# The tail, norm and first block of three chained products, worked by token halves

## The chip, the cores and the metric

One core of a Trainium2 chip. The metric is the device time of one execution in microseconds (us). TensorE is called PE here, VectorE DVE, ScalarE ACT; SP is the engine that issues the weight DMAs.

## The reference

One conditioned decoder layer on 256 tokens of width 2048, in fp32: a SwiGLU FFN (hidden width 5632), a pair of token mixers behind one wide projection, a second FFN, and a last norm. Each of the three sub-layers starts with an RMSNorm that is scaled and shifted by vectors computed from c.

```python
x = x + 1/2 * gate1(c) * SwiGLU1(mod1(RMSNorm(x)))
h = mod2(RMSNorm(x)); p = h @ w_in                 # 2048 x 13312
x = x + gate2(c) * ((sig(g_ret) * y_ret + sig(g_swa) * y_swa) @ w_out)
x = x + 1/2 * gate3(c) * SwiGLU2(mod3(RMSNorm(x)))
out = RMSNorm(x) * norm_final
mod(h) = h * (1 + scale(c)) + shift(c);  [shift, scale, gate] x 3 = c_act @ w_ada + b_ada
SwiGLU(h) = (silu(h @ w_gate) * (h @ w_up)) @ w_down
```

## The kernel before

**Products.** Tokens lie in two halves t of 128. Each fp32 product is three PE matmuls: high part by high part (L288), low by high (L289), high by low (L290). A weight tile is 512 x 512 (1 MB): `load` issues its DMA on SP into one of four `raw` buffers; ACT casts its high part `wh` in two pieces of 128x1024 (L296), and DVE subtracts to get the low part `wl` (L297). The split pieces live in `wsp`, three buffers of each kind. The activation side is split either once for all (`Held`, tiles `hh` and `hl`) or as it is used (`Whole.pair`, tile `a`: ACT L327, DVE L328). `gemm` walks the contraction in steps of four blocks of 128 (a "kb"); for each tile it runs both token halves, 24 matmuls. The down products (ffn1 down, w_out, ffn2 down) are worked in two passes of two column blocks of 512.

**Background.** The vectors for shift, scale and gate come from `ada`: 1 MB of `w_ada` into a `raw` buffer and four DVE reductions (L195) per step. `gemm` starts such steps at the given `rate`, so they stand among the product's own work on DVE and SP.

**Boundaries.** After a down product's second pass, `add_gated` scales each half's PSUM bank (L442), adds it to x (L443) and lets ACT sum its squares (L381). Then one `inv_rms` for both halves (reduce L385, square root on ACT L369, four DVE steps), then `norm`: per 256 columns and half a DVE scaling (L416), PE transposes (L420), a DVE modulation from PSUM (L401, 128x256), ACT's `hh` (L404) and DVE's `hl` (L405). There are two such boundaries, from ffn1 down to w_in and from w_out to the second FFN; behind ffn2 down the last norm writes the output (L895, DMA L903).

**Order.** Every engine runs its own instructions strictly in a fixed order. SP's is the program's; that of the others is set when the kernel is built. An instruction that waits holds up all that stand behind it on its engine.

```python
for p in range(2):
    c0s = [(2 * p + i) * CH for i in range(2)]
    banks = gemm(act, w, c0s, KT=KF, rate=rate)
    for b, c0 in zip(banks, c0s):
        add_gated(b, c0, gate, ssq)
```

## Time and profile before

| | |
|---|---|
| median of 3 runs | 2516.82 us (2515.35 to 2518.6) |
| the profiled execution | 2512.52 us |
| its span | 2510.7 us |
| mean granted PE clock | 0.992 |
| PE busy | 2431.5 us, 97% of the span |
| DVE busy | 1712.6 us, 68% |
| ACT busy | 1172.6 us, 47% |

The span runs from the first to the last instruction that the profile shows; 1.8 us of the profiled execution lie outside it. PE has work in 97% of the span, so what a change can take back on PE's side is idle time and time at a low clock.

### The profile page before, as it was taken

To read this page: it belongs to the slowest core of one execution; us is meant where nothing else is said; L and a number is where in the kernel's file an instruction comes from. 1 tells how busy PE (TensorE), PEld (TensorE's weight loads), DVE (VectorE), ACT (ScalarE), POOL (GpSimd) and SP (SyncE) were. 2 spreads that over 40 slices of the span, in tenths; PEclk is the share of its full clock that TensorE was granted. 3 is DMA by queue.
4 is the path that set the end of the run, shared out by engine and by line. 5 is a ranking of instruction groups with operands and counts; after the bars stand their busy time and mean duration, and the time that the engine had idled before them with its cause. 6 is when DMAs were issued, how large, how long until landed. Compare 5 with 4: busy or idle time off the path is not lost.

```text
span 2510.7 us, 29247 instructions
## 1 busy us (share of the span) xinstructions
PE 2431.5 (97%) x10910; PEld 1977.4 (79%) x10910; DVE 1712.6 (68%) x2843; ACT 1172.6 (47%) x1566; POOL 5.7 (0%) x14
## 2 busy tenths in 40 slices
PE   6999999999997999999999999998999999999997
PEld 4778888788786877777888888886788888888886
DVE  7997776668877766776766776766756554445655
ACT  5445444344444454455444454455444444444443
POOL 0000000000000000000000000000000000000000
PEclk9999999999998999999999999999999999999999
DMA  9995787788786655555667777765566665555553
GB/s 361 361 341 202 250 291 296 278 292 300 268 299 241 230 204 185 194 184 193 226 246 254 246 273 252 280 213 189 184 235 245 225 251 187 197 187 190 196 185 116
DMA packets 243472, 599.08 MB, mean 239 GB/s; under 512 B 9537, under 2 KB 9921, under 8 KB 224001
## 3 DMA queue, kind: packets, MB, share of 16 engines
q1 hardware_dynamic: 242402, 591.61, 66.4%
...
HBM read 595.06 MB, written 2.12 MB: 238 GB/s over the span
## 4 chain that ended last, share of the span: by engine, by line
PE 91%; DVE 6%; DMA 1%; ACT 1%; issue 1%; SPq 0%; ACTq 0%; DVEq 0%
PE pa L290 29%; PE pa L289 29%; PE pa L288 29%; DVE wl L297 2%; PE ps L361 1%; DVE slot L195 1%; DMA raw<-in_w_ada_dram 1%; DVE raw L195 1%; PE pd L639 1%; PE pd L636 0%; ACT wh L296 0%; PE pd L701 0%; PE pd L361 0%; DVE slot L572 0%; DMA x_sb<-in_x_dram 0%
## 5 line engine op out<-in xcount | busy, mean ns | idle before, releaser
L297 DVE TENSOR_TENSOR wl<-raw,wh 128x1024 fp32r<-128x1024 f32 x842 | 1014.0, 1211 | 644.5 <-ACT wh L296 641.5
L296 ACT CAST wh<-raw 128x1024 fp32r<-128x1024 f32 x842 | 878.2, 1043 | 1130.9 <-PE pa L289 1101.3
L289 PE MATMUL pa<-wh,hl 128*128 128x512 f32 x2240 | 878.4, 392 | 1.1 <-DVE hl L405 1.1
L288 PE MATMUL pa<-wh,hh 128*128 128x512 f32 x2240 | 871.0, 393 | 5.6 <-ACT hh L404 2.1
L290 PE MATMUL pa<-wl,hh 128*128 128x512 f32 x2240 | 817.1, 394 | 8.1 <-DVE wl L297 7.7
L290 PEld LDWEIGHTS pa<-wl,hh 128*128 128x128 f32 x2240 | 418.7, 188 | 104.4 <-DVE wl L297 17.2
L288 PEld LDWEIGHTS pa<-wh,hh 128*128 128x128 f32 x2240 | 421.4, 188 | 99.6 <-ACT wh L296 4.5
L289 PEld LDWEIGHTS pa<-wh,hl 128*128 128x128 f32 x2240 | 421.6, 188 | 90.7 <-issue 2.8
L289 PE MATMUL pa<-wh,a 128*128 128x512 f32 x1088 | 423.4, 390 | 3.2 <-DVE a L328 3.2
L288 PE MATMUL pa<-wh,a 128*128 128x512 f32 x1088 | 403.6, 391 | 1.3 <-ACT wh L296 0.9
L290 PE MATMUL pa<-wl,a 128*128 128x512 f32 x1088 | 403.2, 390 | 0.1
L289 PEld LDWEIGHTS pa<-wh,a 128*128 128x128 f32 x1088 | 204.5, 188 | 47.2 <-DVE a L328 4.6
L288 PEld LDWEIGHTS pa<-wh,a 128*128 128x128 f32 x1088 | 204.2, 188 | 45.9 <-ACT wh L296 2.2
L290 PEld LDWEIGHTS pa<-wl,a 128*128 128x128 f32 x1088 | 204.6, 188 | 43.1 <-DVE wl L297 0.9
L195 DVE CUSTOM_DVE_ANT_0 raw<-raw,cact 128x512 f32<-128x512 f32 x336 | 214.6, 687 | 0.0
L195 DVE CUSTOM_DVE_ANT_0 raw<-raw,cact,bcols 128x512 f32<-128x512 f32 x112 | 83.9, 749 | 85.0 <-DMA raw<-in_w_ada_dram 84.8
L328 DVE TENSOR_TENSOR a<-slot,a 128x512 fp32r<-128x512 f32 x136 | 93.1, 685 | 0.0
L327 ACT CAST a<-slot 128x512 fp32r<-128x512 f32 x136 | 83.9, 618 | 0.0
L195 DVE CUSTOM_DVE_ANT_0 slot<-slot,cact 128x512 f32<-128x512 f32 x96 | 61.5, 689 | 0.0
L362 ACT COPY slot<-ps 128x512 f32<-128x512 f32 x80 | 43.9, 588 | 35.4 <-PE ps L361 35.1
L195 DVE DVE_READ_ACCUMULATOR2_ANT sums<- 128x1 f32 x576 | 48.0, 83 | 0.0
L361 PE MATMUL ps<-small_c,t 128*128 128x128 f32 x288 | 38.9, 273 | 0.0
...
## 6 DMA issues: line engine op xcount, KB each, us to landing
raw<-in_w_ffn_gu_dram SPq DMA_DIRECT2D x156, 1024.0 KB, 4.9
raw<-in_w_ada_dram SPq DMA_DIRECT2D x112, 1024.0 KB, 4.9
raw<-in_w_in_dram SPq DMA_DIRECT2D x104, 1024.0 KB, 5.0
raw<-in_w_ffn_down_dram SPq DMA_DIRECT2D x88, 1024.0 KB, 5.1
slot<-in_w_ada_dram SPq DMA_DIRECT2D x32, 1024.0 KB, 8.0
raw<-in_w_swa_branch_dram SPq DMA_DIRECT2D x16, 1024.0 KB, 5.2
raw<-in_w_ret_branch_dram SPq DMA_DIRECT2D x16, 1024.0 KB, 5.3
raw<-in_w_out_dram SPq DMA_DIRECT2D x16, 1024.0 KB, 5.1
```

The lines of the kernel that those rows point to most:

```text
L195: nc.vector.tensor_tensor_reduce(out=w[:, at], in0=w[:, at], in1=cact[:, at], scale=1.0, scalar=bcols[:, m, k : k + 1] if q == 0 else 0.0, ...
L288: nc.tensor.matmul(ps, ah[:, j, ts], wh[:, j, :], start=first, stop=False)
L289: nc.tensor.matmul(ps, al[:, j, ts], wh[:, j, :], start=False, stop=False)
L290: nc.tensor.matmul(ps, ah[:, j, ts], wl[:, j, :], start=False, stop=last)
L296: nc.scalar.copy(hi, src)
L297: nc.vector.tensor_sub(lo, src, hi.bitcast(F32))
L327: nc.scalar.copy(hi, v)
L328: nc.vector.tensor_sub(lo, v, hi.bitcast(F32))
L361: nc.tensor.transpose(ps[:, j * P : (j + 1) * P], src_of(j), ident)
L362: nc.any.tensor_copy(dest, ps[:, : n * P])
L639: nc.tensor.matmul(ps[:, P : 3 * P], qo[hs, pair, P:], skt[hs, kv, :], start=True, stop=True)
```

## The change

The last pass of a down product ends in `gemm_tail`: of its last two steps a and b, the first tile is run whole, and the three others, (a, second column block), (b, first), (b, second), are split but kept: two of them in 16 KB buffers of the slot pool ("home" tiles), the last in `wsp`, and the activations of step b in a home tile as well. Then half 0 of all three is multiplied, then half 1. `add_gated` and the norm follow per half: `norm_half` for the two boundaries, `final` at the end. `gemm_head` does the same for the first block of the next product: its four tiles are kept split (three in homes, the last in `wsp`); half 0 is multiplied as soon as its norm is there, half 1 later. `inv_rms` now takes one half; its square root adds the epsilon by itself, and `root_table` is a square root of a constant in front of each down product. The scaling by the norm is on ACT (L517, 128x512), the modulation alternates by 128 columns between DVE (L531) and ACT (L529), and `hh`/`hl` are made per half for four blocks at once (L537, L538). Some background rates differ (0.55 to 0.6 in the first FFN's up product, 0.36 to 0.375 in w_in, 0.25 to 0 in ffn2 down), and no background step is started in the last two steps of a tail or in a head. The number of matmuls is the same.

```diff
-    def products(banks, ah, al, wh, wl, starts, ends):
+    def products(banks, ah, al, wh, wl, starts, ends, halves=range(NT)):
         n = ah.shape[1]
         for j in range(n):
             first, last = starts and j == 0, ends and j == n - 1
-            for t in range(NT):
+            for t in halves:
...
+        def pair(self, k2, home=None):
             t = self.tiles[k2 * 2 // KD]
             j = (2 * k2) % KD
             v = t.rearrange("p (k s) -> p k s", s=S)[:, j : j + 2, :]
-            both = pair_tile()
+            if home is None:
+                home = pair_tile()
...
+    def home_tile():
+        return slots.tile([P, 2, KD * P], F32R, tag="slot", name=nm("home"))
...
+    def halves_of(w, kb, c0, home=None):
+        raw = load(w, kb, c0)
+        pairs = []
+        for h in range(2):
+            src = raw[:, 2 * h : 2 * h + 2, :]
+            if home is None:
+                pairs.append(split(wsp, "w", src, CH))
+                continue
+            hi, lo = (
+                home[:, i].rearrange("p (k n) -> p k n", n=CH)[:, 2 * h : 2 * h + 2, :]
+                for i in range(2)
+            )
+            nc.scalar.copy(hi, src)
+            nc.vector.tensor_sub(lo, src, hi.bitcast(F32))
+            pairs.append((hi, lo))
+        return pairs
...
+    def gemm_tail(act, w, col0s, KT, rate):
+        banks = [[acc_bank() for _ in range(NT)] for _ in col0s]
+        nb = KT // KB
+        for kb in range(nb - 2):
+            credit[0] += rate * len(col0s)
+            n = int(credit[0])
+            credit[0] -= n
+            gemm_part(act, w, col0s, banks, kb, KT)
+            tick(n)
+        a, b = nb - 2, nb - 1
+        pairs = {a: [act.pair(a * 2 + h) for h in range(2)]}
+        for h, (wh, wl) in enumerate(halves_of(w, a, col0s[0])):
+            products(banks[0], *pairs[a][h], wh, wl, False, False)
+        steps = [(a, 1, halves_of(w, a, col0s[1], home_tile()))]
+        home = home_tile().rearrange("p i n -> p (i n)")
+        pairs[b] = [
+            act.pair(
+                b * 2 + h,
+                home[:, h * 2 * CH : (h + 1) * 2 * CH].rearrange("p (i n) -> p i n", i=2),
+            )
+            for h in range(2)
+        ]
+        steps.insert(0, (b, 0, halves_of(w, b, col0s[0], home_tile())))
+        steps.append((b, 1, halves_of(w, b, col0s[1])))
+        def last(t):
+            for kb, i, parts in steps:
+                for h, (wh, wl) in enumerate(parts):
+                    products(
+                        banks[i], *pairs[kb][h], wh, wl, False, kb == b and h == 1, [t]
+                    )
+        last(0)
+        return banks, lambda: last(1)
...
+    def gemm_head(w, c0, held):
+        banks = [acc_bank() for _ in range(NT)]
+        nb = KD // KB
+        steps = []
+        def products_of(kb, parts, t):
+            for h, (wh, wl) in enumerate(parts):
+                k2 = kb * 2 + h
+                products(
+                    banks, *held.pair(k2), wh, wl, k2 == 0, 2 * k2 + 2 == KD, [t]
+                )
+        for kb in range(nb):
+            parts = halves_of(w, kb, c0, home_tile() if kb < nb - 1 else None)
+            steps.append((kb, parts))
+            products_of(kb, parts, 0)
+        def rest():
+            for kb, parts in steps:
+                products_of(kb, parts, 1)
+        return banks, rest
...
+    def root_table():
+        nc.scalar.activation(small(1, "root"), eps, AF.Sqrt)
...
+    def inv_rms(ssq, t):
+        s = small(1, "sum")
+        v = small(1, "var")
+        r = small(1, "rs1")
+        q = small(1, "rq1")
         nc.vector.tensor_reduce(
-            out=v, in_=ssq.rearrange("p (t c) -> p t c", t=NT), axis=AX.X, op=ALU.add
-        )
+            out=s, in_=ssq[:, t * 4 : (t + 1) * 4], axis=AX.X, op=ALU.add
+        )
+        nc.scalar.activation(r, s, AF.Sqrt, bias=eps, scale=1.0 / D)
...
+        nc.vector.reciprocal(r, r)
+        nc.vector.scalar_tensor_tensor(
+            out=q, in0=v, scalar=r, in1=r, op0=ALU.mult, op1=ALU.mult
+        )
+        nc.vector.tensor_scalar(
+            out=q, in0=q, scalar1=-0.5, scalar2=1.5, op0=ALU.mult, op1=ALU.add
+        )
+        nc.vector.tensor_mul(r, r, q)
+        return r
...
+    def norm_half(held, ssq, t, m_shift):
+        r = inv_rms(ssq, t)
+        ts = slice(t * P, (t + 1) * P)
+        for kb in range(KD // KB):
+            xn = t512()
+            xs = x_sb[:, t, kb * CH : (kb + 1) * CH]
+            nc.scalar.mul(xn, xs, r)
+            ps = bank()
+            h = t512()
+            for j in range(KB):
+                js = slice(j * P, (j + 1) * P)
+                nc.tensor.transpose(ps[:, js], xn[:, js], ident)
+            for j in range(KB):
+                js = slice(j * P, (j + 1) * P)
+                k = kb * KB + j
+                scale = modc[:, m_shift + 1, k : k + 1]
+                shift = modc[:, m_shift, k : k + 1]
+                if j % 2:
+                    nc.scalar.activation(h[:, js], ps[:, js], AF.Identity, bias=shift, scale=scale)
+                else:
+                    nc.vector.tensor_scalar(
+                        out=h[:, js], in0=ps[:, js], scalar1=scale, scalar2=shift,
+                        op0=ALU.mult, op1=ALU.add,
+                    )
+            h4 = h.rearrange("p (k s) -> p k s", s=P)
+            hi = held.hi[:, kb * KB : (kb + 1) * KB, ts]
+            nc.scalar.copy(hi, h4)
+            nc.vector.tensor_sub(
+                held.lo[:, kb * KB : (kb + 1) * KB, ts], h4, hi.bitcast(F32)
...
-    def add_gated(banks, c0, gate, ssq):
+    def add_gated(banks, c0, gate, ssq, halves=range(NT)):
+        for t in halves:
...
-    def ffn_up(held, w, tiles, first, rate):
+    def ffn_up(held, w, tiles, first, rate, bg=None):
         for ci in range(first, DFF // CH):
-            bg = gemm(held, w, [ci * CH], rate=rate)[0]
+            bg = bg or gemm(held, w, [ci * CH], rate=rate)[0]
             bu = gemm(held, w, [DFF + ci * CH], rate=rate)[0]
             swiglu_up(bg, bu, tiles, ci)
-    def ffn_down(tiles, w, gate, rate):
+            bg = None
...
+    def down_product(act, w, gate, KT, rate, half_done):
         ssq = small(NT * 4, "ssq")
-        act = Whole(tiles)
-        for p in range(2):
-            c0s = [(2 * p + i) * CH for i in range(2)]
-            banks = gemm(act, w, c0s, KT=KF, rate=rate)
+        root_table()
+        c0s = [0, CH]
+        banks = gemm(act, w, c0s, KT=KT, rate=rate)
+        for b, c0 in zip(banks, c0s):
+            add_gated(b, c0, gate, ssq)
+        c0s = [2 * CH, 3 * CH]
+        banks, rest = gemm_tail(act, w, c0s, KT, rate)
+        rest()
+        for t in range(NT):
             for b, c0 in zip(banks, c0s):
-                add_gated(b, c0, gate, ssq)
-        return ssq
+                add_gated(b, c0, gate, ssq, [t])
+            half_done(ssq, t)
...
+    def into_norm(m_shift, w):
+        held = Held()
+        box = []
+        def half_done(ssq, t):
+            norm_half(held, ssq, t, m_shift)
+            if t == 0:
+                box.extend(gemm_head(w, 0 if m_shift == 6 else O_SK, held))
+            else:
+                box.pop()()
+        return held, box, half_done
...
-    ffn_up(held, gu, tiles, 5, 0.55)
+    ffn_up(held, gu, tiles, 5, 0.6)
     gate_load(gate, 2)
-    ssq = ffn_down(tiles, dn, gate, 0.55)
-    need(4, 3)
-    held = norm(ssq, 3)
     wi = w_in[0]
+    held, head, half_done = into_norm(3, wi)
+    down_product(Whole(tiles), dn, gate, KF, 0.55, half_done)
+    assert {3, 4} <= done
     dec = one.tile([P, D], F32, tag="row", name="dec")
     nc.gpsimd.dma_start(dec, consts[:, C_DEC:])
-    MR = 0.36
+    MR = 0.375
...
-    b = in_chunk(O_SK)
+    b = head[0]
...
-    for p in range(2):
-        c0s = [(2 * p + i) * CH for i in range(2)]
-        banks = gemm(a_m, w_out[0], c0s)
-        for b, c0 in zip(banks, c0s):
-            add_gated(b, c0, gate, ssq)
     need(7, 6)
-    held = norm(ssq, 6)
+    held, head, half_done = into_norm(6, w_ffn2_gu[0])
+    down_product(a_m, w_out[0], gate, KD, 0.0, half_done)
...
+    ffn_up(held, w_ffn2_gu[0], tiles, 0, 0.25, head[:1][0])
...
+    def final(ssq, t):
+        r = inv_rms(ssq, t)
+        for ci in range(4):
+            cs = slice(ci * CH, (ci + 1) * CH)
             o = t512()
...
+    down_product(Whole(tiles), w_ffn2_down[0], gate, KF, 0.0, final)
```

ACT at the boundary from ffn1 down to w_in. Before, from the table load for the square root on (`rs2` is the inverse RMS of both halves, `t` a modulated block):

```order
L369 ACT_TABLE_LOAD
L369 ACTIVATE rs2_1062_5958<-var_1061_5955 128x2
L404 CAST hh_1064_5966<-t_1069_5977 128x256
L404 CAST hh_1064_5966<-t_1070_5981 128x256
L404 CAST hh_1064_5966<-t_1074_5994 128x256
```

Now, from the table load of half 0 on (`home` and `wh` on the left are high parts of w_in's first block; 1085 is its last tile, 1119 the next block's first; `t_1062`, `t_1065`, `t_1068` are the scaled x; `hh_753` the first high part that PE can use):

```order
L482 ACT_TABLE_LOAD
L482 ACTIVATE rs1_1060_5957<-sum_1058_5955,eps_100 128x1
L377 CAST home_1078_6043<-raw_1079_6044 128x1024 x2
L377 CAST home_1080_6062<-raw_1081_6063 128x1024 x2
L517 ACTIVATE t_1062_5966<-x_sb_91,rs1_1060_5957 128x512
L298 CAST wh_1085_6087<-raw_1082_6081 128x1024
L298 CAST wh_1119_6269<-raw_1118_6267 128x1024
L517 ACTIVATE t_1065_5980<-x_sb_91,rs1_1060_5957 128x512
L529 ACTIVATE t_1064_5969<-ps_1063_5968,modc_129 128x128
L517 ACTIVATE t_1068_5994<-x_sb_91,rs1_1060_5957 128x512
L529 ACTIVATE t_1064_5969<-ps_1063_5968,modc_129 128x128
L537 CAST hh_753_4154<-t_1064_5969 128x4x128
```

Four casts of kept weights (two rows x2) stand between half 0's square root and its first scaling of x, and the first `hh` stands behind two modulations by ACT.

DVE at the same place. Before, from the last step of the inverse RMS on:

```order
L376 TENSOR_TENSOR rs2_1062_5958<-rs2_1062_5958,rq2_1063_5959 128x2
L416 TENSOR_SCALAR t_1067_5969<-x_sb_91,rs2_1062_5958 128x256
L416 TENSOR_SCALAR t_1068_5973<-x_sb_91,rs2_1062_5958 128x256
L401 TENSOR_SCALAR t_1069_5977<-ps_1066_5968,modc_127 128x256
L401 TENSOR_SCALAR t_1070_5981<-ps_1066_5968,modc_127 128x256
L416 TENSOR_SCALAR t_1072_5986<-x_sb_91,rs2_1062_5958 128x256
L416 TENSOR_SCALAR t_1073_5990<-x_sb_91,rs2_1062_5958 128x256
L405 TENSOR_TENSOR hl_1065_5967<-t_1069_5977,hh_1064_5966 128x256
L405 TENSOR_TENSOR hl_1065_5967<-t_1070_5981,hh_1064_5966 128x256
```

Now, from the step behind half 0's inverse RMS on (`home` low parts of the kept tiles, the two modulations of the first four blocks of 128 columns, one background step on `raw_1123`, of which six like rows are left out, and the first `hl`):

```order
L378 TENSOR_TENSOR home_1078_6043<-raw_1079_6044,home_1078_6043 128x1024 x2
L378 TENSOR_TENSOR home_1080_6062<-raw_1081_6063,home_1080_6062 128x1024 x2
L531 TENSOR_SCALAR t_1064_5969<-ps_1063_5968,modc_129 128x128
L299 TENSOR_TENSOR wl_1086_6088<-raw_1082_6081,wh_1085_6087 128x1024
L299 TENSOR_TENSOR wl_1120_6270<-raw_1118_6267,wh_1119_6269 128x1024
L531 TENSOR_SCALAR t_1064_5969<-ps_1063_5968,modc_129 128x128
L197 ISA raw_1123_6301,sums_1022_5717<-raw_1123_6301,cact_105,bcols_119 128x512
...
L197 ISA sums_1022_5717 128x1
L531 TENSOR_SCALAR t_1067_5983<-ps_1066_5982,modc_129 128x128
L538 TENSOR_TENSOR hl_754_4155<-t_1064_5969,hh_753_4154 128x4x128
```

Where before nothing stood between the inverse RMS and the first `hl` but the norm's own rows, there are now four low parts of homes, two of `wl`, and a background step.

ACT in w_out's second pass, at its second step of four. Before (`wh_2349` and `wh_2351` are the two pieces of that step's first tile, `a_2346` and `a_2347` its activations, `t` the sums of squares of the first pass):

```order
L296 CAST wh_2349_12973<-raw_2348_12971 128x1024
L381 ACTIVATE t_2327_12880,ssq_2269_12566<-x_sb_91 128x512
L381 ACTIVATE t_2329_12885,ssq_2269_12566<-x_sb_91 128x512
L296 CAST wh_2351_12989<-raw_2348_12971 128x1024
L327 CAST a_2346_12965<-slot_1943_10622 128x512
L296 CAST wh_2354_13007<-raw_2353_13005 128x1024
```

Now (`wh_2332` and `wh_2334` are that tile's pieces, `a_2329` its first activations; `home_2348` is the kept tile of the third step, second column block; `home_2350` the activations of the fourth step):

```order
L298 CAST wh_2332_12969<-raw_2331_12967 128x1024
L467 ACTIVATE t_2310_12876,ssq_2251_12560<-x_sb_91 128x512
L467 ACTIVATE t_2312_12881,ssq_2251_12560<-x_sb_91 128x512
L377 CAST home_2348_13075<-raw_2349_13076 128x1024 x2
L330 CAST home_2350_13082<-slot_1922_10608 128x512 x2
L298 CAST wh_2334_12985<-raw_2331_12967 128x1024
L330 CAST a_2329_12961<-slot_1922_10608 128x512
L298 CAST wh_2337_13003<-raw_2336_13001 128x1024
```

The casts of a tile two steps ahead and of the last step's activations stand in front of the activations that PE needs next. `raw_2349` is loaded into the buffer that `raw_2324`, the second tile of the step before, leaves free. DVE's rows keep the same order (low parts of `home_2348` and `home_2350`, then `wl_2335`, then `a_2329`).

## Rows read from the trace of the kernel before

**Rows 1.** The page, busy us, share of the span, instructions
```profile
PE 2431.5 (97%) x10910; PEld 1977.4 (79%) x10910; DVE 1712.6 (68%) x2843; ACT 1172.6 (47%) x1566; POOL 5.7 (0%) x14
```

**Rows 2.** Waits of PE: us in total, times, longest
```profile
PE ps L420 <- DVE t L416: 24.6, 3, 14.4
```

**Rows 3.** Stretches: busy (x instructions) of PE, PEld, DVE, ACT, POOL, then PEclk
```profile
790.25:804.70 14.45, 0.03 (x1) 0.06 (x1) 11.95 (x30) 5.23 (x11) 0.53 (x1) 0.61 0.70 242
804.70:840.00 35.30, 33.21 (x148) 26.39 (x149) 28.91 (x64) 15.86 (x25) 0.00 (x0) 0.92 0.36 124
1747.60:1758.90 11.30, 1.09 (x4) 0.72 (x4) 7.80 (x19) 5.53 (x12) 0.00 (x0) 0.72 0.33 120
1758.90:1795.00 36.10, 34.96 (x156) 28.17 (x157) 29.21 (x62) 18.87 (x28) 0.00 (x0) 0.95 0.42 148
2496.04:2510.70 14.66, 0.00 (x1) 0.00 (x0) 8.65 (x19) 3.08 (x8) 0.00 (x0) 0.64 0.39 144
666.00:669.00 3.00, 0.23 (x1) 0.00 (x0) 3.00 (x5) 0.72 (x2) 0.00 (x0) 1.00 0.82 238
669.00:674.00 5.00, 4.96 (x15) 3.93 (x16) 4.15 (x8) 2.21 (x5) 0.00 (x0) 0.66 0.67 277
```

**Rows 4.** A shorter stretch, same columns
```profile
804.70:810.30 5.60, 4.53 (x14) 3.54 (x15) 3.63 (x11) 1.54 (x4) 0.00 (x0) 0.50 0.39 146
```

**Rows 5.** Timeline, ffn1 down to w_in: start, duration, engine, instruction, [idle <-releaser]
```profile
789.86 0.39 PE L290 MATMUL pa<-wl,a 128*128 128x512 f32 x1
...
795.37 0.68 DVE L442 TENSOR_TENSOR t<-pa,row 128x512 f32<-128x512 f32 x1
...
798.14 0.63 ACT L381 ACTIVATE t<-x_sb 128x512 f32<-128x512 f32 x1 [0.60 <-DVE x_sb L443]
...
800.03 0.75 DVE L195 CUSTOM_DVE_ANT_0 raw<-raw,cact,bcols 128x512 f32<-128x512 f32 x1 [1.92 <-DMA raw<-in_w_ada_dram]
...
804.67 1.09 PE L420 MATMUL ps<-small_c,t 128*128 128x128 f32 x4 [14.42 <-DVE t L416]
...
806.37 0.86 ACT L404 CAST hh<-t 128x256 fp32r<-128x256 f32 x2 [3.23 <-DVE t L401]
...
806.83 1.22 PE L288 MATMUL pa<-wh,hh 128*128 128x512 f32 x2 [1.07 <-ACT hh L404]
...
808.55 0.78 PE L289 MATMUL pa<-wh,hl 128*128 128x512 f32 x1
```

**Rows 6.** Timeline, w_out to ffn2: the norm's chain
```profile
1753.74 1.28 ACT L369 ACT_TABLE_LOAD   x1
...
1755.03 0.20 ACT L369 ACTIVATE rs<-var 128x2 f32<-128x2 f32 x1
```

**Rows 7.** Timeline, w_out, second pass
```profile
1706.45 1.22 DVE L297 TENSOR_TENSOR wl<-raw,wh 128x1024 fp32r<-128x1024 f32 x1
...
1713.49 0.61 ACT L327 CAST a<-slot 128x512 fp32r<-128x512 f32 x1
...
1714.16 0.73 PE L288 MATMUL pa<-wh,a 128*128 128x512 f32 x2
...
1715.67 0.39 PE L289 MATMUL pa<-wh,a 128*128 128x512 f32 x1
```

**Rows 8.** DMA issues, KB and us to landing: all of w_out; the one at 1707.69
```profile
raw<-in_w_out_dram SPq DMA_DIRECT2D x16, 1024.0 KB, 5.1
...
raw<-in_w_out_dram SPq DMA_DIRECT2D x1, 1024.0 KB, 6.5
```

**Rows 9.** Timeline, the end
```profile
2498.72 0.19 ACT L381 ACTIVATION_READ_ACCUMULATOR t<-x_sb 128x1 f32 x1
...
2501.44 5.46 DVE L895 SCALAR_TENSOR_TENSOR t<-x_sb,rs,slot 128x512 f32<-128x512 f32 x8
```

**Rows 10.** The page, groups: mean ns of one before the second bar
```profile
L297 DVE TENSOR_TENSOR wl<-raw,wh 128x1024 fp32r<-128x1024 f32 x842 | 1014.0, 1211 | 644.5 <-ACT wh L296 641.5
L296 ACT CAST wh<-raw 128x1024 fp32r<-128x1024 f32 x842 | 878.2, 1043 | 1130.9 <-PE pa L289 1101.3
```

More of the change, by code (lines that the diff above doesn't have):

```diff
@@ L156, in layer_kernel @@
     nc.sync.dma_start(x_sb[:, 1, :], x[0, P:, :])
+    eps = one.tile([P, 1], F32, tag="eps", name="eps")
+    nc.vector.memset(eps, EPS)
     ones = t512()[0:1, :P]
@@ L322, in pair @@
             v = t.rearrange("p (k s) -> p k s", s=S)[:, j : j + 2, :]
-            both = pair_tile()
+            if home is None:
+                home = pair_tile()
             hi, lo = (
-                both[:, i].rearrange("p (k s) -> p k s", k=2).bitcast(F32R) for i in range(2)
+                home[:, i].rearrange("p (k s) -> p k s", k=2).bitcast(F32R) for i in range(2)
             )
@@ L523, in layer_kernel @@
         )
-    r = inv_rms(ssq)
+    r = [inv_rms(ssq, t) for t in range(NT)]
     bounds = (0, 2, 5, 8, 12, 16)
@@ L886, in layer_kernel @@
     gate_load(gate, 8)
-    ssq = ffn_down(tiles, w_ffn2_down[0], gate, 0.25)
-    r = inv_rms(ssq)
-    for ci in range(4):
-        cs = slice(ci * CH, (ci + 1) * CH)
-        for t in range(NT):
+    def final(ssq, t):
+        r = inv_rms(ssq, t)
+        for ci in range(4):
+            cs = slice(ci * CH, (ci + 1) * CH)
             o = t512()
@@ L897, in layer_kernel @@
                 in0=x_sb[:, t, cs],
-                scalar=r[:, t : t + 1],
+                scalar=r,
                 in1=gf[:, cs],
```

36 lines of the change are left out of this document (2 added, 34 removed).

## The prediction

> **What bounds the kernel now.** I read the page first: PE is busy 97% of the span, DVE 68%, ACT 47% [rows 1]. The change leaves the number of matmuls alone, so only PE's idle time and its time at the lower clock can pay. PE's waits grouped by releaser come next: 24.6 us of them end with DVE's scaling of x by the inverse RMS, in three waits, the longest 14.4 us [rows 2]. The timeline shows where: at the two boundaries at which a down product meets a norm. At the first (ffn1 down to w_in) the last matmul starts at 789.86, the first transpose at 804.67, the first product 16.6 us behind the last one's end (790.25 to 806.83), and the first with a low part at 808.55 [rows 5]. The stretches give the idle time: 14.42 us plus 35.30 - 33.21 = 2.09, together 16.5 us; at the second boundary 10.21 + 1.14 = 11.35 us [rows 3]. A background step on DVE (from 800.03) lies within the first boundary's chain and not within the second's, which is most of the difference [rows 5]. After the restart the granted clock is 0.50 for 5.6 us, with PE busy for 4.53 of them, so about 2.3 us are lost to the lower level, 1.2 instead of 2.4 GHz [rows 4]. Behind the last matmul the kernel needs 14.66 us of norm and output [rows 3]. These 42 us and their clock loss of about 5 are all that the change addresses.
>
> **The change, part by part.** E is PE's last matmul of the down product. A matmul costs 2431.5/10910 = 0.22 us [rows 1]. In the new order half 0 of the tail ends 29 matmuls before E, at E - 6.5.
>
> *First boundary.* The chain of half 0: scaling and adding of one column block about 1.4 (two take 2.77, 795.37 to 798.14), the square 0.63 [rows 5] and its sum 0.19 [rows 9], table load 1.28 and root 0.20 [rows 6], the other steps of the inverse RMS 1.05 (2498.91 to 2501.44 is 2.53, less load and root) [rows 9]. That is 4.75, so the root is done at about E - 2.8 and the inverse RMS at E - 1.75. Were nothing in front, x would be scaled before E. But four casts of kept w_in tiles stand ahead of the scaling on ACT, 4 x 1.04 [rows 10], to E + 1.4, and the scaling (0.63, as the square) ends at E + 2. On DVE four low parts at 1.21 [rows 10] end at E + 3.1. Then the order alternates: DVE modulation, two `wl` at 1.21, DVE modulation, ACT modulation, `hh`. The trace has no 128x128 modulation; the nearest row is an `hh` of twice the width, 0.43 (0.86 for two) [rows 5]. I take 0.35 for each (0.2 to 0.45) and 0.43 for the new `hh`. The first product can start at E + 7.0. The first `hl` stands behind another background step (four reductions, the first 0.75 [rows 5], together some 2.6), so the first low-part product starts at E + 9.5. Before, these were E + 16.6 and E + 18.3. Idle time after: 7.0 less 0.6 for four transposes; 0.8 between the two starts (four matmuls at half clock fill 1.7 of 2.5); about 1.3 while blocks two to four pass the same alternation; 1.5 until half 1's norm is there (my choice between 0, if half 0's products, 48 x 0.22 = 10.6 us, cover it, and 4, a norm chain of its own); 0.5 in the tail. Together 10.5, against 16.5: **-6 us** (3 to 8). The clock loss stays, since PE still waits about 7 us.
>
> *Second boundary.* The same rows stand there without the background step before `hl`: 6.4 + 1.5 + 0.5 + 0.5 = 8.9 against 11.35: **-2.5** (1 to 4).
>
> *w_out's tail.* With four steps only, the kept tiles come early. In the second pass ACT casts the kept tile `home_2348` and the last step's activations before the `a_2329` that PE needs for its second step. Before, that `a` was cast at 1713.49 and PE went on at 1714.16, low part at 1715.67 [rows 7]. The kept tile's buffer is freed by the `wl` that ends at 1707.67 [rows 7], and its load lands 5.1 us later by w_out's median, or 6.5 as that very issue did [rows 8]: 1712.8 to 1714.2. From landing, ACT takes 2 x 1.04 + 2 x 0.61 + 1.04 + 0.61 = 4.95 [rows 7, 10]; DVE's low part of `a_2329`, behind two low parts of the home, two of activations and a `wl`, ends some 6.8 behind the landing. PE then goes on at 1719.6 to 1721.0 instead of 1715.67: 3.9 to 5.3 us that nothing gives back. A wait of 2.8 us elsewhere, within the stretch from 666, left the clock at 0.66 of full over 5 us, 1.7 us lost [rows 3]. I take 4.5 + 1.5: **+6** (3.9 to 7).
>
> *The end.* Half 0's norm and root, its table load too, run under half 1's matmuls; DVE finishes half 0's outputs 0.6 behind E. Then two column blocks 2.8, square and sum 0.8, inverse RMS 0.2 + 1.05, four outputs at 0.6 (5.46 for eight, 0.68 each [rows 9]), and 3.8 from the last output's end to the end of the span (2510.70 - 2506.90 [rows 3, 9]): 11.9 against 14.66, -2.75. A cast of a kept tile also stands ahead of weights in this tail, +0.7: **-2** (1 to 3.5). The table load left out here is worth 1.28, since the root starts at 1755.03 behind a load that ends at 1755.02 [rows 6]. The Trainium skill ("ScalarE: Activation LUTs", What ACT_TABLE_LOAD costs) puts a drain of some 1.4 us beside each load, 2.66 in all; by it the end would save 1.4 us more and the sum be 5.3. The rows show no such drain, so I keep 1.28.
>
> *The start.* A table load for the constant's root and several small DVE steps per half in place of both at once: **+0.6** (0 to 1), bounded by one load of 1.28 [rows 6], part of it under the loads of x.
>
> *At nothing* stand the other edits: the changed background rates and the missing background in tails and heads move DVE work that PE does not wait for while DVE is 68% busy (up to 2 either way if a `wl` comes late), and the split of ACT and DVE work over the norm counts in the chains above.
>
> The sum is -6 - 2.5 + 6 - 2 + 0.6 = -3.9 us. The profiled execution is 2512.52, which becomes 2508.6; it is 4.3 under the median of the runs, so I forecast a median of 2516.8 - 3.9 = 2512.9, **2513 us**.
>
> **The rivals.**
>
> *No stall in w_out* (faster). If the kept tile lands early enough, or PE is itself late there, the +6 is gone: -9.9, 2507. For it: PE must be just 4 us behind. Against: the casts stand ahead in ACT's fixed order, and the load cannot start before 1707.7.
>
> *Full cover* (faster). Half 0's products start at once and half 1 hides behind them: the idle time at both boundaries falls to about 2 each and the clock holds, -14.5 - 9.4 - 4.5 + 6 - 2 + 0.6, some 24 us: 2493. Against it: the four casts in front of the scaling, which no faster arithmetic moves.
>
> *The alternation is slower than the products* (slower). The norm of a block of four goes ACT, PE, DVE, ACT, DVE, ACT, ACT, DVE, one waiting for the other. PE uses up a half block in 12 x 0.22 = 2.7 us. There are 16 such blocks at the two boundaries. If each takes 0.6 us more than 2.7, the 9.6 us reach beyond the -3.9 by more than 5; at 1.0 more, less the 3.8 already counted, it is +12 - 3.9: about 2525. For it: eight hand-overs, with weights' casts and low parts in between. Against: the scaling of a later block stands early in ACT's rows, so blocks overlap.
>
> *The change moves the wait only* (no change). The boundary costs what it did since the casts and low parts now in the chain take the place of the second half's work: -2 at the end alone, 2515.
>
> **How the numbers follow.** Forecast 0.50, no stall 0.24, full cover 0.05, alternation 0.12, moved wait 0.09. A measurement tells a difference from none at about 0.2%, 5 us here: below 2511.8 is faster, above 2521.9 slower. The forecast's own range, 2508 to 2518 from its bounds, lies with 0.13 under 2511.8 and 0.37 within. Faster: 0.13 + 0.24 + 0.05 = 0.42; same 0.37 + 0.09 = 0.46; slower 0.12. The range takes in the no-stall case with room for its bounds and ends before full cover and the slow alternation: 2502 to 2521.
>
> **What the profile after would show.** Right: PE's idle time at the first boundary about 10, its wait ending with ACT's `hh` and then DVE's `hl`; four `home` casts between the root and the first scaling; in w_out's second pass a PE wait of some 4 us on `a`, and a lower clock behind it; 12 us behind the last matmul. Wrong, if that w_out wait is missing or another kept tile stalls its product as this one does (in ffn1 or ffn2), or if half 0's products at a boundary run in pieces.

## The result, and the profile after

| | before | after | ratio (95%) |
|---|---|---|---|
| first chip, 20 runs each | 2515.18 us | 2519.03 us | 1.0016 (1.0009 to 1.0023) |
| again on another chip, 24 and 12 runs (e8) | 2511.47 us | 2512.79 us | 1.0008 (0.9998 to 1.0018) |

The change makes the kernel 3.85 us slower on the first chip and 1.3 us on the second (an interval that takes in no change at all), where 3.9 us less was forecast. The profiled execution of after (2524.87 us, span 2522.6) is the longest of its 20 runs, so e8 stands beside it below. But e8's is the longest of its 12 too (2518.73), and before's (2512.52) lies 2.7 us under its median of 20, so these profiles lie further apart than the medians.

The page, engines and the two groups of [rows 10]:

```profile
PE 2446.1 (97%) x10910; PEld 1982.7 (79%) x10910; DVE 1700.4 (67%) x2814; ACT 1194.3 (47%) x1610; POOL 5.6 (0%) x14
...
L299 DVE TENSOR_TENSOR wl<-raw,wh 128x1024 fp32r<-128x1024 f32 (+1 forms) x818 | 984.6, 1210 | 617.1 <-ACT wh L298 615.0
L298 ACT CAST wh<-raw 128x1024 fp32r<-128x1024 f32 (+1 forms) x818 | 852.0, 1042 | 1121.2 <-PE pa L291 1063.9
```

Waits of after: five of PE's over the span, then one of DVE's from 180 to 545, nearly all of the first FFN's up product (us in total, times, longest):

```profile
PE pa L292 <- DVE wl L299: 13.8, 16, 3.1
PE ps L522 <- ACT t L517: 8.2, 5, 2.5
PE pa L291 <- DVE a L331: 6.3, 6, 3.0
PE ps L522 <- ACT t L529: 4.9, 4, 1.6
PE pa L290 <- ACT a L330: 3.4, 1, 3.4
...
DVE raw L197 <- DMA raw<-in_w_ada_dram: 58.2, 23, 5.6
```

The same wait of DVE before (reductions at L195 there), then PE's two on low parts:

```profile
DVE raw L195 <- DMA raw<-in_w_ada_dram: 48.8, 20, 5.2
...
PE pa L290 <- DVE wl L297: 7.7, 11, 1.5
PE pa L289 <- DVE a L328: 3.2, 3, 2.8
```

And in e8:

```profile
DVE raw L197 <- DMA raw<-in_w_ada_dram: 41.3, 23, 4.4
...
PE pa L291 <- DVE a L331: 9.5, 6, 4.1
PE pa L292 <- DVE wl L299: 6.6, 10, 1.3
```

The 24.6 us in which PE waited for the scaling [rows 2] have become 8.2 + 4.9, none over 2.5. But PE's waits on low parts, of weights (`wl`) and activations (`a`) together, have grown from 10.9 us to 20.1, and to 16.1 in e8. Stretches of after (columns as in [rows 3]):

```profile
371.00:378.20 7.20, 7.20 (x33) 5.94 (x32) 1.66 (x2) 2.49 (x3) 0.00 (x0) 1.00 0.99 381
379.00:386.00 7.00, 3.99 (x12) 3.21 (x13) 5.44 (x10) 1.04 (x1) 0.00 (x0) 0.82 0.59 209
807.36:843.00 35.64, 27.22 (x113) 21.34 (x113) 23.45 (x49) 21.51 (x40) 0.53 (x1) 0.81 0.42 148
1725.00:1735.00 10.00, 6.63 (x18) 4.50 (x18) 7.26 (x9) 7.26 (x10) 0.00 (x0) 0.67 0.54 184
2510.59:2522.60 12.01, 0.00 (x0) 0.00 (x0) 7.18 (x16) 1.74 (x5) 0.00 (x0) 0.62 0.45 167
```

Timeline of after: the up product, the first boundary, w_out's second pass, the second boundary, the end:

```profile
369.28 0.37 SPq L275 DMA_DIRECT2D raw<-in_w_ffn_gu_dram  x1
370.42 0.34 SPq L194 DMA_DIRECT2D raw<-in_w_ada_dram  x1
372.69 0.37 SPq L275 DMA_DIRECT2D raw<-in_w_ffn_gu_dram  x1
378.22 0.75 DVE L197 CUSTOM_DVE_ANT_0 raw<-raw,cact,bcols 128x512 f32<-128x512 f32 x1 [5.56 <-DMA raw<-in_w_ada_dram]
380.73 3.49 DVE L299 TENSOR_TENSOR wl<-raw,wh 128x1024 fp32r<-128x1024 f32 x3
380.84 0.34 SPq L194 DMA_DIRECT2D raw<-in_w_ada_dram  x1
382.01 0.74 PE L292 MATMUL pa<-wl,hh 128*128 128x512 f32 x2 [3.09 <-DVE wl L299]
383.11 0.37 SPq L275 DMA_DIRECT2D raw<-in_w_ffn_gu_dram  x1
385.78 0.75 DVE L197 CUSTOM_DVE_ANT_0 raw<-raw,cact,bcols 128x512 f32<-128x512 f32 x1 [1.56 <-DMA raw<-in_w_ada_dram]
...
803.78 1.28 ACT L482 ACT_TABLE_LOAD   x1
805.08 0.30 ACT L482 ACTIVATE rs<-sum,eps 128x1 f32<-128x1 f32 x1
805.28 3.88 ACT L377 CAST home<-raw 128x1024 fp32r<-128x1024 f32 x4
806.97 0.39 PE L292 MATMUL pa<-wl,home 128*128 128x512 f32 x1
809.05 0.72 ACT L517 ACTIVATE t<-x_sb,rs 128x512 f32<-128x512 f32 x1
815.20 0.78 PE L290 MATMUL pa<-home,hh 128*128 128x512 f32 x1
817.51 0.80 PE L291 MATMUL pa<-home,hl 128*128 128x512 f32 x1 [1.53 <-DVE hl L538]
...
1727.07 1.13 ACT L330 CAST home<-slot 128x512 fp32r<-128x512 f32 x2
1729.06 0.61 ACT L330 CAST a<-slot 128x512 fp32r<-128x512 f32 x1
1729.72 2.17 PE L290 MATMUL pa<-wh,a 128*128 128x512 f32 x4 [3.37 <-ACT a L330]
...
1764.90 0.39 PE L292 MATMUL pa<-wl,home 128*128 128x512 f32 x1
1772.45 0.79 PE L290 MATMUL pa<-home,hh 128*128 128x512 f32 x1
```

At the first boundary the four casts stand between root and scaling, as forecast, and the first product starts 7.84 us behind the last one's end (807.36 to 815.20), the first low part 10.15; before it was 16.6 and 18.3 [rows 5]. In w_out PE waits 3.37 us for `a`, with the clock at 0.67 around it. The end takes 12.01 us against 14.66 [rows 3]. All this was forecast in kind; the loss lies ahead of it.

To see where, I cut each profiled execution at E1, E2 and E3, the ends of the last matmuls (start + 0.39) of ffn1 down, w_out and ffn2 down; d1 is the start of ffn1 down's first product. In us:

| kernel | d1 | d1 to E1 | 0 to E1 | E1 to E2 | E2 to E3 | E3 to end |
|---|---|---|---|---|---|---|
| before | 543.1 | 247.2 | 790.25 | 957.3 | 748.5 | 14.7 |
| after | 554.9 | 252.5 | 807.4 | 957.9 | 745.3 | 12.0 |
| e8, after again | 542.4 | 256.9 | 799.3 | 958.0 | 747.1 | 12.1 |
| e1, before with the new rates | 546.4 | 252.6 | 799.0 | 953.8 | 749.4 | 14.7 |
| e2, after with rates put back | 543.5 | 256.4 | 800.0 | 960.3 | 745.9 | 12.1 |
| e3, w_out's order | 543.7 | 253.2 | 796.9 | 951.5 | 744.5 | 12.2 |
| e4, norm first | 546.3 | 251.5 | 797.8 | 961.5 | 749.1 | 12.1 |
| e5, first boundary as before | 540.7 | 249.9 | 790.6 | 956.7 | 744.3 | 12.1 |
| e6, steps spread | 546.0 | 251.8 | 797.8 | 951.3 | 743.1 | 12.1 |
| e7, before with steps spread | 546.9 | 250.4 | 797.3 | 955.2 | 750.7 | 14.7 |
| e9, reductions late | 539.5 | 253.4 | 792.9 | 959.9 | 744.4 | 12.1 |
| e10, before with late reductions | 537.8 | 256.3 | 794.1 | 963.5 | 749.2 | 14.7 |
| e11, reductions late in up | 539.1 | 252.4 | 791.5 | 952.7 | 745.0 | 12.2 |
| e12, e5 and late reductions | 539.6 | 250.3 | 789.9 | 954.9 | 745.3 | 12.1 |
| e13, e11 and seam | 538.0 | 249.7 | 787.7 | 954.4 | 744.7 | 12.2 |
| e14, e6 and late reductions | 539.0 | 249.9 | 788.9 | 950.2 | 745.5 | 12.1 |

Up to E1 after is 17.1 and 9.0 us longer than before, in the up product or in ffn1 down. The stretches, up product before and after, then ffn1 down before and in e8 (columns as in [rows 3]):

```profile
180.00:543.09 363.09, 359.35 (x1624) 296.75 (x1623) 259.76 (x427) 164.23 (x189) 1.07 (x2) 1.00 0.74 268
180.00:554.88 374.88, 365.43 (x1624) 299.49 (x1623) 265.83 (x444) 164.18 (x189) 1.06 (x2) 0.99 0.75 267
...
543.09:790.25 247.16, 243.66 (x1065) 199.64 (x1063) 196.27 (x333) 118.66 (x141) 0.00 (x0) 0.99 0.81 289
542.42:799.28 256.86, 246.92 (x1065) 201.53 (x1063) 196.63 (x325) 124.15 (x150) 0.00 (x0) 0.98 0.78 274
```

After's up product is 11.8 us longer, 5.7 of it PE's idle time (9.4 against 3.7) and 6.1 slower matmuls, whose clock falls behind the waits (0.59 from 379 to 386). e8's ffn1 down is 9.7 us longer, 6.4 of it idle (9.9 against 3.5) and 3.3 slower matmuls.

### The profile page after: what moved, and what is told of

Same layout as the page of the kernel before. It is cut to its first block, busy times and chain, and to the rows that moved or that the text cites. A ratio compares the mean times of both kernels' runs of the same rounds, so it can differ in the third digit from the quotient of the medians.

```text
span 2522.6 us, 29243 instructions
## 1 busy us (share of the span) xinstructions
PE 2446.1 (97%) x10910; PEld 1982.7 (79%) x10910; DVE 1700.4 (67%) x2814; ACT 1194.3 (47%) x1610; POOL 5.6 (0%) x14
## 4 chain that ended last, share of the span: by engine, by line
PE 86%; DVE 7%; DMA 4%; ACT 2%; issue 1%; DVEq 0%; SPq 0%; ACTq 0%
PE pa L292 27%; PE pa L291 27%; PE pa L290 27%; DMA raw<-in_w_ada_dram 4%; DVE wl L299 2%; DVE raw L197 2%; PE ps L447 1%; DVE slot L197 1%; PE pd L767 1%; ACT wh L298 0%; PE pd L764 0%; PE pd L829 0%; PE pd L447 0%; DVE slot L700 0%; DVE home L378 0%
## 5 line engine op out<-in xcount | busy, mean ns | idle before, releaser
L299 DVE TENSOR_TENSOR wl<-raw,wh 128x1024 fp32r<-128x1024 f32 (+1 forms) x818 | 984.6, 1210 | 617.1 <-ACT wh L298 615.0
L298 ACT CAST wh<-raw 128x1024 fp32r<-128x1024 f32 (+1 forms) x818 | 852.0, 1042 | 1121.2 <-PE pa L291 1063.9
L290 PE MATMUL pa<-wh,hh 128*128 128x512 f32 x2192 | 859.4, 394 | 3.4 <-ACT wh L298 1.9
L291 PE MATMUL pa<-wh,hl 128*128 128x512 f32 x2192 | 860.7, 393 | 0.0
L292 PE MATMUL pa<-wl,hh 128*128 128x512 f32 x2192 | 799.5, 395 | 13.7 <-DVE wl L299 13.4
L292 PEld LDWEIGHTS pa<-wl,hh 128*128 128x128 f32 x2192 | 409.6, 189 | 110.9 <-DVE wl L299 23.9
L291 PE MATMUL pa<-wh,a 128*128 128x512 f32 x1016 | 398.0, 393 | 6.4 <-DVE a L331 6.3
L290 PE MATMUL pa<-wh,a 128*128 128x512 f32 x1016 | 379.4, 394 | 4.6 <-ACT a L330 3.4
L292 PE MATMUL pa<-wl,a 128*128 128x512 f32 x1016 | 378.6, 392 | 0.5 <-DVE wl L299 0.4
L291 PEld LDWEIGHTS pa<-wh,a 128*128 128x128 f32 x1016 | 192.1, 189 | 49.8 <-DVE a L331 10.1
L290 PEld LDWEIGHTS pa<-wh,a 128*128 128x128 f32 x1016 | 191.5, 189 | 48.0 <-ACT a L330 5.3
L292 PEld LDWEIGHTS pa<-wl,a 128*128 128x128 f32 x1016 | 191.8, 189 | 40.9 <-DVE wl L299 1.4
```

The source lines that it names most:

```text
L290: nc.tensor.matmul(ps, ah[:, j, ts], wh[:, j, :], start=first, stop=False)
L291: nc.tensor.matmul(ps, al[:, j, ts], wh[:, j, :], start=False, stop=False)
L292: nc.tensor.matmul(ps, ah[:, j, ts], wl[:, j, :], start=False, stop=last)
L298: nc.scalar.copy(hi, src)
L299: nc.vector.tensor_sub(lo, src, hi.bitcast(F32))
```

## The experiments

My theory was that the first FFN's background steps cost PE time: a change of rates and a tail that takes no steps put them where a late load or two steps in a row hold DVE. The rivals were that the halves' own instructions cost it (tail, homes, norms per half), and, for the boundary, that the casts of kept tiles set it. Runs of one block shared a chip and the runs of before on it.

**Block 1** (before: 2512.27 us).

*e1*: the kernel before, with two of the change's rates alone.

```diff
-    ffn_up(held, gu, tiles, 5, 0.55)
+    ffn_up(held, gu, tiles, 5, 0.6)
...
-    MR = 0.36
+    MR = 0.375
```

> The kernel before with only two background rates of the change: 0.6 instead of 0.55 in the first FFN's up product, 0.375 instead of 0.36 in w_in. Theory A (the rate of background steps costs the time in the first FFN: a background tile lands late, DVE stands in front of it, the low parts behind it come late for PE): slower than before by 5 to 12 us, with two or more PE waits of about 3 us on wl between 350 and 560 and a DVE wait of over 4.5 us on the background DMA ahead of each. Rival B (the rates cost nothing, the other edits shift the first FFN): within 3 us of before.

2513.73 us, 1.0007 (0.9998 to 1.0016). E1 comes 8.7 us later in its profile (the longest of its 12 executions), but the wait behind E1 shrinks from 16.6 to 13.3 us and E1 to E2 from 957.3 to 953.8: the rates alone decide nothing that can be measured in the total.

*e2*: the changed kernel, with the rates the other way.

```diff
-    ffn_up(held, gu, tiles, 5, 0.6)
+    ffn_up(held, gu, tiles, 5, 0.55)
...
-    down_product(Whole(tiles), dn, gate, KF, 0.55, half_done)
+    down_product(Whole(tiles), dn, gate, KF, 0.58, half_done)
...
-    MR = 0.375
+    MR = 0.36
```

> The change with the rates put back: 0.55 in the first FFN's up product, 0.36 in w_in, and 0.58 (0.55 in both kernels) in ffn1 down, so that the same number of background steps is done ahead of the boundary. Theory A: the end of ffn1 down comes at about 792 us instead of 807, and the time is 5 to 10 us under the change's, so about 2 to 6 under before. Rival B (the per-half start and root table shift the first FFN, not the rates): as the change, about 4 us over before.

2516.17 us, 1.0014 (1.0005 to 1.0024): no gain. The steps that the tail does not take now stand in ffn1 down, 256.4 us long against 247.2, and the first product starts E1 + 14.63.

*e3*: the casts and low parts of the kept tiles in a tail are ordered behind the activations of the step before (an order on the engine, no wait).

```diff
+        with tc.issue_after(hi_before), tc.issue_after(lo_before):
-        steps = [(a, 1, halves_of(w, a, col0s[1], home_tile()))]
+            steps = [(a, 1, halves_of(w, a, col0s[1], home_tile()))]
...
```

> The change, with ACT's and DVE's rows for the kept tail tiles put behind the activations of the step before the last two (order alone, no work changed; in ffn1 the order stays as it was). Theory A (the casts of a tile that has not landed hold up the activations that PE needs): the PE wait of 3.4 us near 1730 goes, with the low clock behind it; 4.5 to 6.5 us under the change. Rival B (the late tile stalls PE a little later instead): within 2 us of the change.

2507.07 us, 0.9978 (0.9969 to 0.9986). E1 to E2 falls from 957.9 and 958.0 to 951.5. w_out alone, from the last transpose ahead of it to E2, in after and in e3 (columns as in [rows 3]):

```profile
1680.26:1765.29 85.03, 81.45 (x345) 65.72 (x344) 53.84 (x63) 45.56 (x62) 0.00 (x0) 0.96 0.55 187
...
1668.71:1748.42 79.71, 79.16 (x345) 64.18 (x344) 53.48 (x63) 45.36 (x62) 0.00 (x0) 1.00 0.60 200
```

It takes 79.7 us, not 85.0 (85.2 in e8; before 79.7): the stall is worth 5.3 to 5.5 us. The other 1.1 of the 6.5 lie ahead of it, where this edit changes nothing. In e3's timeline the `a` that PE needs is cast ahead of the home:

```profile
1714.29 0.61 ACT L331 CAST a<-slot 128x512 fp32r<-128x512 f32 x1
...
1714.96 0.73 PE L290 MATMUL pa<-wh,a 128*128 128x512 f32 x2
...
1716.28 1.99 ACT L379 CAST home<-raw 128x1024 fp32r<-128x1024 f32 x2
```

*e4*: the changed kernel; each later kept tile of a head is split behind the norm's `hh` and `hl` of the block before.

```diff
-            parts = halves_of(w, kb, c0, home_tile() if kb < nb - 1 else None)
...
+                hi, lo = held.made[kb - 1]
+                with tc.issue_after(hi), tc.issue_after(lo):
+                    parts = halves_of(w, kb, c0, home_tile() if kb < nb - 1 else None)
```

> The change, with the casts and low parts of the kept head tiles of blocks two to four each put behind the first half's hh and hl of the block before (order alone). Theory A (the casts in front of the scaling are the wait): the first product at both boundaries starts about 2 us behind the last of the down product instead of 7.5, and the time is 5 to 10 us under the change's. Rival B (ACT and DVE have that work to do in the same stretch anyway, so PE waits between blocks instead): within 2 us of the change.

2516.43 us, 1.0021 (1.0010 to 1.0032). The first product starts E1 + 3.25, 4.6 us sooner, and the time comes back further on (e4's timeline):

```profile
801.07 0.50 PE L290 MATMUL pa<-home,hh 128*128 128x512 f32 x1 [0.20 <-ACT hh L543]
...
818.22 0.79 PE L290 MATMUL pa<-wh,hh 128*128 128x512 f32 x1 [5.79 <-ACT hh L543]
```

Ahead of that `hh` DVE works from 805.71 to 817.62 without a pause, on a background step and three `wl` among others, before it comes to the modulation that ACT needs. E1 to E2 is 961.5 and E2 to E3 749.1, each longer than after's (this execution, 2522.55 us, is the second longest of its 12). So the order of the first rows alone only moves the wait; whether another order of the later rows would pay was not tried.

**Block 2** (before: 2511.47 us).

*e5*: e3 with ffn1 down and its norm as before and rates 0.55 and 0.36; halves only from w_out on.

```diff
...
-    held, head, half_done = into_norm(3, wi)
-    down_product(Whole(tiles), dn, gate, KF, 0.55, half_done)
...
+    ssq = ffn_down(tiles, dn, gate, 0.55)
+    need(4, 3)
+    held = norm(ssq, 3)
...
```

> The kernel before in the first FFN and its norm (rates too; only the start's inverse RMS per half is new), the change with the corrected order of the third run in w_out, the second FFN and the end. Theory C (the change lengthens ffn1 down, since background steps fall on other steps of it; the rest of the change pays): ffn1 down ends at 790 to 793 us as before, w_out to the end is as in the third run, and the time is 6 to 9 us under before, though the first boundary's gain of about 6 is given up. Rival D (the per-half start or chance shifts the first FFN): ffn1 down ends at 797 or later and the time is within 3 us of before.

2504.40 us, 0.9971 (0.9959 to 0.9983). E1 is back at 790.6. So the halves' instructions at the start cost nothing to be seen in E1, and without its first boundary and with w_out mended the change gains. Tail, homes, head and rates of the first FFN are all gone here at once, so this run doesn't tell which of them cost the time.

*e6*: e3 with one background step for each step of ffn1 down, from a fixed phase of the counter on.

```diff
-    ffn_up(held, gu, tiles, 5, 0.6)
+    ffn_up(held, gu, tiles, 5, 0.625)
...
+    credit[0] = 0.0
-    down_product(Whole(tiles), dn, gate, KF, 0.55, half_done)
+    down_product(Whole(tiles), dn, gate, KF, 0.5, half_done)
```

> The third run's kernel (the change with w_out's order corrected) with the background steps spread so that each step of ffn1 down gets exactly one (rate 0.5 for two column blocks, the counter set to zero ahead of it, 0.625 in the up product ahead). Theory C (two background steps in a row in ffn1 down are what lengthens it): the PE waits on a near 558 and 674 go or halve, ffn1 down takes 247 us or less instead of 253, and the time is 4 to 8 us under the third run's. Rival D: ffn1 down takes 251 or more, the time within 3 us of the third run's.

2504.16 us, 0.9968 (0.9956 to 0.9980): no different from e3 within the intervals. Its ffn1 down takes 251.8 us: at its start DVE waits 4.50 and 2.02 us for late loads (547.63 and 557.99), and PE behind it 1.63 and 2.17.

*e7*: the same spreading (0.625, 0.0, 0.5) in the kernel before.

> The kernel before with the same spreading of background steps (0.625, then exactly one per step of ffn1 down) and nothing else. Theory C: the wait of 2.8 us at 669 goes too, 2 to 6 us under before. Rival D: within 2 us of before.

2515.75 us, 1.0019 (1.0011 to 1.0028): spreading by itself does not help the kernel before.

*e8*: the changed kernel again, unaltered.

> The change itself once more, beside the others on one chip: its profiled execution was the longest of its twenty runs. 3 to 5 us over before; in a middling execution ffn1 down should end at 796 to 800 us, not at 807, and the second half of the kernel should be as in the first profile.

2512.79 us, 1.0008. Its profile has the up product's d1 at 542.4, not 554.9, but ffn1 down at 256.9. The loss stands in the up product in one execution and in ffn1 down in the other.

**Block 3** (before: 2513.01 us).

*e9*: e3 with each background tile reduced one step later, behind the low parts of the next step's first tile. Its load stays where it was.

```diff
-            ada(m, k, sums)
+            ada(m, k, sums, later=True)
...
+            if i == 0 and pending:
+                with tc.issue_after(getattr(low[0], "ins", low[0])):
+                    flush()
             tick(ticks)
```

> The third run's kernel (the change with w_out's order corrected), where each background step's four reductions are traced one step later and queued on DVE behind the low parts of the next step's first tile; the load is issued where it was. DVE then reaches them some 5 us later, when the tile has landed. Theory E (in the first FFN DVE waits up to 5.6 us for background tiles that land late, with the low parts that PE needs queued behind; this is what grew): DVE's waits for background loads fall from about 70 us to under 20 up to the end of ffn1 down, the PE waits on wl and a there nearly go, ffn1 down ends at 782 to 790 us instead of 797, and the time is 6 to 12 us under the third run's. Rival F (the loads themselves and the four buffers are the limit; a tile that waits longer holds a buffer longer): the wait moves to late weight tiles, time within 3 us of the third run's or above it.

2512.21 us, 1.0003 (0.9994 to 1.0012). No wait of DVE on these loads is left from 180 to 545, and d1 is 539.5. But E1 to E2 takes 959.9 against e3's 951.5: in w_in it costs, from its boundary on (first product at E1 + 11.90, in e3 E1 + 7.07).

*e10*: the same in the kernel before.

> The kernel before with the same later reductions and nothing else. Theory E: 3 to 8 us under before, less than in the run beside it since its first FFN waited less. Rival F: within 3 us of before, or above it.

2522.97 us, 1.0040 (1.0028 to 1.0053): d1 537.8, and E1 to E2 963.5 against 957.3.

**Block 4** (before: 2512.52 us).

*e11*: e9's reductions late only in the first FFN's up product.

```diff
-        if later:
+        if later and lagged[0]:
...
+    lagged[0] = True
     ffn_up(held, gu, tiles, 5, 0.6)
+    lagged[0] = False
```

> The third run's kernel with the later background reductions of the ninth only in the first FFN's up product (there they took PE's waits away; in w_in they cost). Theory E (in the up product DVE's wait for late background tiles is the loss): the first matmul of ffn1 down starts at about 540 us instead of 544 to 546, w_in to the end is as in the third run, 2 to 5 us under the third run's time and 7 to 11 us under before. Rival F (what is won in the up product is lost again in ffn1 down, where the steps then fall): ffn1 down ends at 797 again, within 1.5 us of the third run's ratio.

2503.17 us, 0.9965 (0.9951 to 0.9979); this interval and e3's overlap. Of DVE's waits from 180 to 545 this is the first row in e11, and no row has `in_w_ada_dram`; PE has no wait on `wl` there:

```profile
DVE wl L315 <- ACT wh L314: 88.7, 77, 2.5
```

ffn1 down stays long (252.4). Its timeline at the seam between the two passes, with PE's longest wait there:

```profile
660.19 0.75 DVE L211 CUSTOM_DVE_ANT_0 raw<-raw,cact,bcols 128x512 f32<-128x512 f32 x1 [0.20 <-DMA raw<-in_w_ada_dram]
...
664.44 0.75 DVE L211 CUSTOM_DVE_ANT_0 raw<-raw,cact,bcols 128x512 f32<-128x512 f32 x1
...
668.09 0.69 DVE L348 TENSOR_TENSOR a<-slot,a 128x512 fp32r<-128x512 f32 x1
...
668.83 0.79 PE L307 MATMUL pa<-wh,a 128*128 128x512 f32 x1 [5.25 <-DVE a L348]
```

Two background steps (660.19 and 664.44) stand on DVE ahead of the `a` that PE needs, by the phase of the counter that doles them out.

*e12*: e5 with the same late reductions.

> The fifth run's kernel (first FFN and its norm as before, halves only from w_out on) with the same later reductions in the up product. Theory E: 2 to 4 us under the fifth run's time. Beside the run before it, it tells whether the first boundary by halves pays at all: if it takes 6 us from the boundary and costs 4 to 8 in ffn1 down, the two come out within 3 us of each other.

2503.91 us, 0.9967 (0.9955 to 0.9980), no different from e11: at these rates the first boundary by halves gives nothing net.

**Block 5** (before: 2511.49 us).

*e13*: e11, with the counter set so that the two steps part.

```diff
+    credit[0] = 0.5
     down_product(Whole(tiles), dn, gate, KF, 0.55, half_done)
```

> The eleventh run's kernel with the counter of background steps set to 0.5 ahead of ffn1 down, at the same rate 0.55: the step of ffn1 down that gets two background steps is then in the middle of a pass and no longer at the seam between its two passes, where DVE also has the sums of the first pass. Theory G (two background steps at the seam are what makes ffn1 down longer in the change than before): the PE wait on a at the seam falls from 5.3 us to about 2.7, ffn1 down takes 248 to 250 us instead of 251.7 and the time is 2 to 5 us under the eleventh run's. Rival H (the kept tail or chance): within 1.5 us of it.

2502.59 us, 0.9966 (0.9954 to 0.9978). The seam in e13's timeline has one step, and PE waits 2.52 us:

```profile
657.86 0.75 DVE L211 CUSTOM_DVE_ANT_0 raw<-raw,cact,bcols 128x512 f32<-128x512 f32 x1
...
663.99 0.80 PE L307 MATMUL pa<-wh,a 128*128 128x512 f32 x1 [2.52 <-DVE a L348]
```

ffn1 down falls to 249.7 us, by 2.7, as much as the wait. The total doesn't follow: the first product now starts E1 + 13.56, not 7.35 as in e11. On DVE low parts of kept tiles and two `wl` now stand between the last steps of half 0's inverse RMS (790.66 to 794.26), which in e11 follow each other (789.20 to 789.65).

*e14*: e6 with e11's late reductions (0.625, 0.0 and 0.5 as in e6).

> The sixth run's kernel (one background step in each step of ffn1 down) with the later reductions of the eleventh in the up product. Theory G: as the run before it, within 2 us of it, with one wait on a at the seam of 3 us or less; the late tile that cost 3.8 us at the start of ffn1 down in the sixth run is gone. Rival H: ffn1 down takes 251 us or more again.

2496.89 us, 0.9941 (0.9930 to 0.9953), the fastest of all: 14.6 us under before. Its runs (2494.75 to 2498.59) lie wholly under e13's (2500.16 to 2504.95) on the same chip. The seam wait is 2.50 us, ffn1 down 249.9 and the first product at E1 + 7.53. From e6 it differs in the late reductions alone, and the two intervals lie apart (e6: 0.9956 to 0.9980): in this kernel they are worth 0.27%, some 7 us.

## Why the prediction was wrong

The step that failed is "the changed background rates and the missing background in tails and heads move DVE work that PE does not wait for while DVE is 68% busy (up to 2 either way if a `wl` comes late)", which stands at nothing. The other terms, taken from the table:

- First boundary and w_in, forecast -6: E1 to E2 without w_out is 872.9 (after), 872.8 (e8) and 871.8 (e3) against 877.6 before, -4.8 to -5.8. The first product starts at E1 + 7.84 and the first low part at E1 + 10.15, where 7.0 and 9.5 were forecast, and PE's idle time in the row from 807.36 is 8.4 us (10.5 forecast). But part of this came by luck: the rates alone bring E1 to E2 to 953.8 from 957.3 (e1), and the forecast had them at nothing.
- w_out's tail, +6: 85.0 and 85.2 against 79.7 in e3, +5.3 and +5.5. The forecast had the wait at 3.9 to 5.3 us; it was 3.37, and the clock behind it took the other 2.
- Second boundary and ffn2's tail, -2.5 + 0.7: 745.3 and 747.1 against 748.5, -3.2 and -1.4.
- The end, -2.75: -2.6 (12.0 and 12.1 against 14.7). Its terms as written add up to 11.65, not 11.9; with the row's 0.68 for an output they give 12.0. The Trainium skill ("ScalarE: Activation LUTs", What ACT_TABLE_LOAD costs) would have it save 1.4 us more, by a drain beside each load; after's rows have none (load over at 805.06, root at 805.08).
- The start, +0.6: the first wait of PE for a `wh` behind 40 us comes at 51.8 us on the mean of the twelve profiles with halves at the start, at 51.2 in the four without. Single ones differ by up to 1.9, so this only agrees with the forecast.

The first four make -4.8 + 5.4 - 2.3 - 2.6 = -4.3 us. The medians say +3.85 and +1.3, so what lies ahead of E1 costs 8.1 and 5.6 us more, not 0.6. (These sums mix medians with single profiles, so I trust them to some 3 us.)

What the runs showed in place of that step: DVE works strictly in order, and a background step stands in its order whether or not its tile has landed. At 378.22 DVE had waited 5.56 us for a load issued at 370.42, 7.8 us before. When it was issued, the load of 369.28 was still under way; the DMA engines were 0.99 busy at 381 GB/s. The next such load, issued at 380.84, also had another issued 2.3 us behind it but none just ahead, and was used 4.9 us later (385.78). The Trainium skill ("Perfetto Trace Analysis", Roofline) puts the ceiling of a core's 16 DMA engines at about 435 GB/s; by it the two loads of 1.05 MB issued at 369.28 and 370.42 take 4.8 us at least, an estimate; in the trace, with a third load behind them, both are there 8.9 us after the first issue. Then the three low parts behind the reductions are late, and PE waits 3.1 us. A busy share of 67 or 68% says nothing of this: the 615 us in which DVE waits for ACT's `wh`, and ACT mostly for PE, are idle time to it just like the 58 us in which work that PE needs stands behind a load.

With late reductions DVE's waits on these loads and PE's on `wl` are gone from the up product (e11), and d1 lies between 537.8 and 539.6 in all six profiles with them (e9 to e14), against 540.7 to 554.9 in the ten without. That is shown, and e14 against e6 shows that it reaches the total. But before has such waits too (48.8 us against 58.2 in after and 41.3 in e8), only PE came through with 1.5 us at the longest: what the change adds is not clearly more waiting of DVE, but waits at places where PE runs out of work. Rates and tail each move them: the rates alone make E1 later by 8.7 us (e1), and with the up product's rate put back and ffn1 down's raised the changed kernel has E1 later by 9.7 (e2); both profiles lie 4 to 5 us above their kernels' medians.

In ffn1 down PE waits on `a` in the same way. In e8 DVE waits 2.92 and 0.99 us for two background loads (550.35 and 555.08), and PE 3.46 us behind them (559.47). The steps that the tail doesn't take stand in the up product and in ffn1 down's earlier steps, and in the change's phase of the counter two of them meet at the seam. PE waits there 5.25 us in e11, 3.03 in after and 4.05 in e8, against 2.8 before [rows 3]; moving the phase alone brings 2.52 and ffn1 down from 252.4 to 249.7 (e13). That cause is shown for the seam of e11; in after and e8 the seam is the smaller part of what ffn1 down loses.

Of the prediction's rivals none came true as told: w_out stalled, the boundaries fell short of full cover, and both gained, so neither the alternation nor a moved wait made the kernel slower. Of those to my theory, that the halves' own instructions cost the time ahead of E1 falls with e13 and e14: they have them all and reach E1 at 787.7 and 788.9, no later than e12 (789.9), which has late reductions too but no halves in its first FFN beyond the start. The casts in front of the scaling do set the start of the first product (e4), but taking them away there doesn't pay. The signs listed for right came, but for one: at the first boundary PE's idle time ends mostly with ACT's `t` ahead of the transposes (8.2 and 4.9 us over both boundaries), not with `hh`. Of those for wrong none came: the waits in ffn1 stand behind background steps, not behind a kept tile.

Open stays why one kernel's executions differ by up to 12 us, and why e14 gains over e11: by the profiles 2.6 us up to E1 and 2.5 from E1 to E2, though the first boundary begins alike in both. That e13's boundary begins late because of DVE's order there is my reading and was not tried.
